# The first stage of a transformer layer kernel: both streams begun together, and the conditioning rows made by products

## The chip, the cores and the metric

The kernel runs on one NeuronCore of one Trainium2 chip. Its time is the device time of one execution in microseconds; three executions before the change took 1682.93, 1684.46 and 1685.36 us, so the median is 1684.46 us. A separate execution was profiled.

## The reference

One layer of a hybrid block works on 256 latent tokens `x` and 256 context tokens `ctx`, each of 2048 channels, in fp32. The part that matters here is its beginning: two conditioning vectors, `c` and `c_ctx`, go through silu and the matrix `w_ada` (2048 x 12288), which gives shift and scale for each stream; each stream is normed, scaled and shifted, and then multiplied by `w_in`.

```
sh1, sc1, ...    = split(silu(c) @ w_ada + b_ada, 6)
sh1c, sc1c, ...  = split(silu(c_ctx) @ w_ada + b_ada, 6)
h_l = modulate(rms_norm(x, norm1_w), sh1, sc1)
h_c = modulate(rms_norm(ctx, norm1_w), sh1c, sc1c)
... = split(h_l @ w_in),  split(h_c @ w_in)
x_new = x + g1 * merge(h_l, gla(...), diff_attention(...))
return x_new + g2 * conv_ffn(modulate(rms_norm(x_new, norm2_w), sh2, sc2))
```

What follows (a gated linear attention, a differential attention, the merge and a convolutional feed-forward net) is touched by neither diff nor order.

## The kernel before, in words

Activations lie with channels on the partitions: 16 tiles of 128 channels by 256 tokens for each stream. A product in fp32 is made of rounded halves: `hi` is the value rounded to fp32r, `lo` the rest, and hi*hi + hi*lo + lo*hi are summed.

The first stage runs 16 steps, one for each tile k of channels. A step needs shift and scale of its 128 channels for both streams. `ada_rows` gets them from PE: 16 products of the silu columns `ccol_s` with a 2 MB tile of `w_ada` (four loads `ada` of 512 KB), then a copy to SBUF on ACT (L525, tile `row`), two transposes on PE (L534) and, in `ada_cols`, three small operations on DVE (L536 to L538). `stage` then makes hi and lo of the normed tile: a scaling of x on DVE (L550), the rounding on ACT (L552), the difference on DVE (L556), for stream 0 (tile names `a`) and stream 1 (`c`). The step's part of `w_in`, 128 x 896 (`wraw<-in_w_sw`), is split into `whi` on ACT (L210) and `wlo` on DVE (L217). PE then multiplies: four row products of 128 tokens (`sweep_row`, banks 0 to 3, 512 columns), and three column products (`sweep_col`, banks 4 to 6, 256 columns for each stream). All of these stand in line L374 (`pinned`), so the tile names tell them apart. The ada products of step k+1 stand after the first row product of step k, and what follows from them is done while PE ends step k.

For three of the sixteen tiles (7, 11 and 15, `DOT_TILES`) shift and scale are not made on PE but by dots on DVE (`run_dots`, L412) of transposed tiles of `w_ada` (`ada<-in_w_ad1t`, 512 KB each) with a row of conditioning values that stands on all partitions: `cb` for stream 0, `cbc` for stream 1. The dots of steps 2 to 5 serve tile 7. `cb` is made by `cond_row`: full fp32 products of a broadcast column of `ccol_s` with the identity, copied from PSUM (L590). `cbc` is made another way: 1 MB of `c_ctx` is loaded by a broadcast (128 times the same row), ACT makes its silu factor in three operations a half (L433 to L435), and POOL multiplies (L436).

Before the steps stands the norm: squares of x on ACT and DVE (L491, L493), partly added on DVE (L497, L498), summed over channels by full fp32 products with `ones`, and the root on ACT and DVE (L511 to L515). Stream 0 is loaded, normed and multiplied first; stream 1 follows while step 0 is under way, so `cond_row` and the sums of squares are spread between the products of step 0.

The order on each engine in this stage is the order of the code (`keep_in_program_order`); behind it a scheduler orders the rest. All loads of the stage go through SP's queue (L346) in the order of the code, at most eight at a time; a load also waits until its buffer is free. The ada loads share a ring of 11 buffers (`SLOTS`), the w_in tiles one of four.

Of the kernel before, what the change touches and what calls it, by code (L numbers as in the profile page):

```python
# [44 lines left out]
LATE_ADA = {13: 1, 14: 2}  # L45
GATE_ADA = [0.25] * 4 + [0.5] * 16 + [1] * 12
# [30 lines left out]
def _lay_out(i):  # L77
# [6 lines left out]
    a["c_ctx"] = np.ascontiguousarray(np.asarray(i["c_ctx"])[None])  # L84
# [66 lines left out]
def layer_kernel(tc, I, out):  # L151
# [3 lines left out]
    with es:  # L155
# [213 lines left out]
        with tc.tile_pool(name="first", bufs=1) as p1:  # L369
# [54 lines left out]
            silu_steps = []  # L424

            def load_ctx_row():

                ordered_dma(cbc, I["c_ctx"].to_broadcast([P, D]))
                for q in range(2):
                    x = cbc[:, q * 1024:(q + 1) * 1024]  # L430
                    t = p1.tile([P, 1024], F32, tag="ada", bufs=SLOTS, name="silu")
                    silu_steps.extend([
                        lambda x=x, t=t: kept(S.activation(t, x, AF.Exp, scale=-1.0)),  # L433
                        lambda x=x, t=t: kept(S.activation(t, t, AF.Ln, bias=1.0)),
                        lambda x=x, t=t: (kept(S.activation(t, t, AF.Exp, scale=-1.0)),  # L435
                                          kept(G.tensor_tensor(x, x, t, op=ALU.mult)))])  # L436

# [14 lines left out]
            load_x(0)  # L452
            load_ada(0)
            load_sweep(0)
            load_x(1)

# [11 lines left out]
            logs = kept(act_table("natural_log_exp_and_others", silus))  # L468
            b1 = p1.tile([P, KT], F32, name="b1")
# [38 lines left out]
            def root(s, o):  # L508

                z, t = z1[:, s * T:(s + 1) * T], p1.tile([P, T], F32, tag="zt", bufs=2, name="zt")  # L510
# [75 lines left out]
            ss = sweep[4][:, :T], sweep[2][:, :T]  # L586
            rows = sweep[0], sweep[5], sweep[3], sweep[3]

            def cond_copy(q, copy):
                kept(copy(cb[:, q * 512:(q + 1) * 512], rows[q]))  # L590

            for q in range(2):
                cond_row(q, rows[q])
            for j in range(2):
                squares(0, j)
                added_squares(0, j)
                summed_squares(0, j, ss[0], j == 0, False, 1)
            squares(0, 2)
            squares(0, 3)
            added_squares(0, 2)  # L600
            summed_squares(0, 3, ss[0], False, False, 4)
            summed_squares(0, 2, ss[0], False, True, 1)
            for q in range(2):
                cond_copy(q, S.copy)
            root(0, ss[0])
            row, lows = ada_rows(0), []
            ws = sweep_splits(0, lows)
            m = ada_cols(0, row)
            cond_row(2, rows[2])
            stage(0, m, (0,), lows)  # L610
            for t in range(2):
                sweep_row(0, ws[0], t)
            for g in range(3):
                sweep_col(0, ws[1], g, (0,))
            for j in range(4):
                squares(1, j)
                if j < 3:
                    added_squares(1, j)
                summed_squares(1, j, ss[1], j == 0, j == 3, 1 if j < 3 else 4)
            cond_copy(2, V.tensor_copy)  # L620
            cond_row(3, rows[3])
            root(1, ss[1])
            cond_copy(3, S.copy)
            stage(0, m, (1,))
            row, lows = ada_rows(1), []
            load(2)
            load_ctx_row()
            nxt = sweep_splits(1, lows)
            sweep_row(0, ws[0], 2)
            m = ada_cols(1, row)  # L630
            sweep_row(0, ws[0], 3)
            stage(1, m, lows=lows)
            for g in range(3):
                sweep_col(0, ws[1], g, (1,))
            for k in range(1, KT):
# [4 lines left out]
                if k + 1 < KT:  # L640
                    load_halves(k + 1)
# [20 lines left out]
                for g in range(3):  # L662
                    sweep_col(k, ws[1], g)
# [774 lines left out]
```

## Time and profile before

| | |
|---|---|
| median of three executions | 1684.46 us |
| the profiled execution | 1686.63 us |
| its span | 1684.8 us |
| PE busy | 1662.6 us (99%) |
| DVE, ACT, POOL busy | 1308.4, 983.6, 349.3 us |
| first stage, to the last product of step 15 | 138.3 us |
| moved by DMA | 371.87 MB, mean 221 GB/s |

A row of the timeline has the start and length in us, the engine, the line of the kernel, the operation, what it writes and reads with shapes, how many were merged into the row, and in brackets how long the engine was idle before it and what ended that. PE's matmuls are pipelined, so one lasts longer than the distance to the next one; the distance of the starts is what a product costs. A product in full fp32 shows as two records.

### The profile page before, as it was taken

Reading aid. Unit: us, or ns where it says so; the run is one execution under the profiler, and the core shown is the slowest. Engines: PE = TensorE matmul, PEld = TensorE weight load, DVE = VectorE, ACT = ScalarE, POOL = GpSimd, SP = SyncE. Lnnn points to the kernel's source line nnn. Section 1 sums busy time; section 2 is a strip of 40 time slices with the busy share of each in tenths; the row PEclk is TensorE's granted clock in tenths of the full one; section 3 lists DMA queues with packets and bytes.
Section 4 is the critical chain, followed back from the end, with each engine's and each line's share of the span. In section 5 each row is a group of like instructions: output and inputs, shape, how many; then the busy total and the mean of one; then the engine's idle time right before and its main releaser. Section 6 shows DMA issues by size and latency. Waiting matters only on the chain.

```text
span 1684.8 us, 28432 instructions
## 1 busy us (share of the span) xinstructions
PE 1662.6 (99%) x10006; PEld 1436.7 (85%) x10006; DVE 1308.4 (78%) x2480; ACT 983.6 (58%) x1983; POOL 349.3 (21%) x442
## 2 busy tenths in 40 slices
PE   7999999999999999999999999999999999999998
PEld 5679999998788888888888998888888888888887
DVE  5788867768787988788998797878888787755655
ACT  5335555756355777666665686666666666544443
POOL 0101313132210000001324200222222222684000
PEclk9999999999999999999999999999999999999999
DMA  9996644436554555687887666677777776676664
GB/s 384 406 376 195 219 151 137 143 101 213 175 188 152 179 192 191 205 291 272 271 269 249 183 200 219 226 228 236 240 236 236 226 239 214 207 219 208 217 194 143
DMA packets 110975, 371.87 MB, mean 221 GB/s; under 512 B 14448, under 2 KB 19568, under 8 KB 110704
## 3 DMA queue, kind: packets, MB, share of 16 engines
q1 hardware_dynamic: 102256, 363.56, 65.1%
q10 hardware_dynamic: 4032, 4.37, 0.8%
q0 software_dynamic: 4544, 2.14, 0.6%
q8 instruction: 78, 1.28, 0.3%
q14 instruction: 65, 0.53, 0.1%
HBM read 365.78 MB, written 2.10 MB: 218 GB/s over the span
## 4 chain that ended last, share of the span: by engine, by line
PE 95%; DVE 2%; DMA 1%; issue 1%; ACT 1%; DVEq 0%; ACTq 0%
PE down L1390 14%; PE upg L268 9%; PE upv L268 9%; PE gate L268 7%; PE upv L270 5%; PE upg L270 5%; PE sweep L374 5%; PE gate L270 4%; PE mix L268 4%; PE mix L270 2%; PE pgb L268 2%; PE pga L268 2%; PE dk L339 2%; PE dk L338 2%; PE dk L337 2%; PE dvb L285 2%
## 5 line engine op out<-in xcount | busy, mean ns | idle before, releaser
L210 ACT CAST whi<-wraw 128x512 fp32r<-128x512 f32 (+2 forms) x1004 | 605.7, 608 | 391.0 <-DVE wlo L217 111.5
L217 DVE TENSOR_TENSOR wlo<-wraw,whi 128x512 fp32r<-128x512 f32 (+2 forms) x932 | 639.1, 694 | 222.2 <-ACT whi L210 209.1
L268 PE MATMUL upg<-a,whi 128*128 128x512 f32 x656 | 229.0, 391 | 0.0
L268 PE MATMUL upv<-a,whi 128*128 128x512 f32 x656 | 228.9, 391 | 0.0
L1390 PE MATMUL down<-whi,g 128*128 128x512 f32 x704 | 216.9, 389 | 0.0
L270 PE MATMUL upv<-a,wlo 128*128 128x256 f32 x656 | 183.0, 280 | 0.0
L270 PE MATMUL upg<-a,wlo 128*128 128x256 f32 x656 | 182.8, 280 | 0.0
L217 POOL TENSOR_TENSOR wlo<-wraw,whi 128x512 fp32r<-128x512 f32 x72 | 100.6, 1397 | 387.6 <-ACT whi L210 379.1
L268 PE MATMUL gate<-a,whi 128*128 128x512 f32 x512 | 179.8, 397 | 0.0
L362 DVE CUSTOM_DVE_ANT_0 araw<-araw,cb 128x1024 f32<-128x1024 f32 x128 | 161.6, 1265 | 13.8 <-DMA araw<-in_w_ada 13.8
L1390 PEld LDWEIGHTS down<-whi,g 128*128 128x128 f32 x704 | 132.1, 188 | 27.5
L268 PEld LDWEIGHTS upv<-a,whi 128*128 128x128 f32 x656 | 122.3, 187 | 26.4
L268 PEld LDWEIGHTS upg<-a,whi 128*128 128x128 f32 x656 | 122.4, 187 | 26.4
L270 PE MATMUL gate<-a,wlo 128*128 128x256 f32 x512 | 140.0, 284 | 0.0
L1390 PE MATMUL down<-wlo,g 128*128 128x512 f32 x352 | 137.0, 389 | 0.0
L270 PEld LDWEIGHTS upv<-a,wlo 128*128 128x128 f32 x656 | 124.1, 189 | 0.5
L270 PEld LDWEIGHTS upg<-a,wlo 128*128 128x128 f32 x656 | 124.1, 189 | 0.5
L268 PEld LDWEIGHTS gate<-a,whi 128*128 128x128 f32 x512 | 94.4, 188 | 19.6 <-issue 0.7
L270 PEld LDWEIGHTS gate<-a,wlo 128*128 128x128 f32 x512 | 96.5, 188 | 5.6 <-issue 1.8
L268 PE MATMUL mix<-a,whi 128*128 128x512 f32 x256 | 88.8, 397 | 0.0
L1390 PEld LDWEIGHTS down<-wlo,g 128*128 128x128 f32 x352 | 66.1, 188 | 13.6
L1363 POOL DMA_DIRECT2D row<-turned x128 | 69.3, 550 | 28.3 <-DVE turned L1359 16.7
(361 smaller groups left out, 3448.4 us busy)
## 6 DMA issues: line engine op xcount, KB each, us to landing
wraw<-in_w_up SPq DMA_DIRECT2D x164, 512.0 KB, 4.5
araw<-in_w_ada SPq DMA_DIRECT2D x128, 512.0 KB, 5.0
wraw<-in_w_down SPq DMA_DIRECT2D x88, 512.0 KB, 4.3
wraw<-in_w_gate SPq DMA_DIRECT2D x64, 512.0 KB, 4.5
wraw<-in_w_in SPq DMA_DIRECT2D x58, 512.0 KB, 4.3
ada<-in_w_ad SPq DMA_DIRECT2D x52, 512.0 KB, 9.8
wraw<-in_w_proj SPq DMA_DIRECT2D x32, 512.0 KB, 4.7
wraw<-in_w_out SPq DMA_DIRECT2D x32, 512.0 KB, 4.8
```

The source lines that it names most:

```text
L210: copied[0] = S.copy(hi[:, :n], raw)
L217: i = e.tensor_tensor(lo[:, :n], raw, hi[:, :n].bitcast(F32), op=ALU.subtract)
L268: i = PE.matmul(b.rearrange("p (a b) -> p a b", a=2), whi[:, sl], acts[k], start=first, stop=last)
L270: i = PE.matmul(b[:, T:], wlo[:, sl], acts[k][:, 1, :], start=False, stop=last)
L285: return PE.matmul(o, hi[k][:, ts], wlo[:, sl], start=False, stop=last)
L337: PE.matmul(o, whi[:, sl], hi[k], start=first and j == 0, stop=False)
L338: PE.matmul(o, whi[:, sl], lo[k], start=False, stop=False)
L339: i = PE.matmul(o, wlo[:, sl], hi[k], start=False, stop=last and j == 1)
L362: i = V.tensor_tensor_reduce(raw, raw, cb[:, q * 1024:(q + 1) * 1024], 1.0, 0.0, op0=ALU.mult, op1=ALU.add, accum_out=ada2[:, j, q:q + 1])
L374: return kept(PE.matmul(*args, **kw))
L1363: nc.gpsimd.dma_start(to[32 * (q % 4):32 * (q % 4 + 1), :, 32 * p:32 * (p + 1)], turned[32 * p:32 * (p + 1), :, 32 * q:32 * (q + 1)])
L1390: i = PE.matmul(banks[h][t][n], g[:, a, ts], w[n][b], start=k == 0 and (a, b) == (1, 0), stop=k == FT - 1 and b == 1)
```

## The change

Stream 1 is loaded right behind stream 0 and ahead of the first ada tiles; both are normed together, with one root over 512 columns, and step 0 is run for both streams like any other. The row `cbc` is no longer loaded: it is made like `cb`, by products with the identity, from the silu column of stream 1. These products are now made with rounded operands: the column is split into `chi` and `clo`, and each is multiplied by the rounded identity `identr`, so there are 64 rounded products where there were 16 in full fp32. The eight results are copied to `cb` and `cbc` by ACT and DVE. The three silu steps of each half on ACT and the two products on POOL are gone. A table `ROWS_AT` says after how many of a step's seven products the ada products of the next step stand: four in steps 0 and 1, two in step 2, one in the others; the transposes stand two products later, at most before the sixth.

On SP the order of the loads was this (`x` the streams, `ada` the tiles of `w_ada`, `wraw` those of `w_in`):

```order
L346 DMA x<-in_xl 128x1024 x4
L346 DMA ada<-in_w_ad 128x1024 x4
L346 DMA wraw<-in_w_sw 128x896
L346 DMA x<-in_xc 128x1024 x4
L346 DMA ada<-in_w_ad 128x1024 x4
L346 DMA wraw<-in_w_sw 128x896 x2
L346 DMA ada<-in_w_ad 128x1024 x4
L346 DMA cbc<-in_c_ctx 128x2048
L346 DMA wraw<-in_w_sw 128x896
```

and now:

```order
L346 DMA x<-in_xl 128x1024 x4
L346 DMA x<-in_xc 128x1024 x4
L346 DMA ada<-in_w_ad 128x1024 x4
L346 DMA wraw<-in_w_sw 128x896
L346 DMA ada<-in_w_ad 128x1024 x4
L346 DMA wraw<-in_w_sw 128x896 x2
L346 DMA ada<-in_w_ad 128x1024 x4
L346 DMA wraw<-in_w_sw 128x896
```

The ctx tiles moved ahead of five loads, and the broadcast row is gone; the rest of SP's order is as it was.

On PE the program began like this (`sweep_133` to `139` are banks 0 to 6, `ab` the bank of the ada products):

```order
L374 MATMUL sweep_133<-ident,ccol_s 128x128 x4
L374 MATMUL sweep_138<-ident,ccol_s 128x128 x4
L374 MATMUL sweep_137<-sq,ones 128x256 x7
L374 MATMUL ab<-ada,ccol_s 32x256 x16
L534 MATMUL ab<-ident,row 128x128 x2
L374 MATMUL sweep_136<-ident,ccol_s 128x128 x4
L374 MATMUL sweep_133<-whi,a_222 128x512
L374 MATMUL sweep_133<-wlo,a_222 128x512
```

Now 48 rounded products on six banks stand first (the last two are shown; banks are 139 to 145), then the sums of both streams, 16 more rounded products on banks 2 and 3, and the ada products. This is the end of that piece:

```order
L374 MATMUL sweep_145<-identr,chi 128x128
L374 MATMUL sweep_145<-identr,clo 128x128
L374 MATMUL sweep_143<-sq,ones 128x256 x14
L374 MATMUL sweep_141<-identr,chi 128x128
L374 MATMUL sweep_141<-identr,clo 128x128
...
L374 MATMUL ab<-ada,ccol_s 32x256 x16
L526 MATMUL ab<-ident,row 128x128 x2
L374 MATMUL sweep_139<-whi,a_313 128x512
L374 MATMUL sweep_139<-wlo,a_313 128x512
```

Everything PE has to do for both norms and all conditioning rows now stands ahead of the first row product. On POOL two products left the queue, with nothing else moved; before:

```order
L471 TENSOR_SCALAR b_129<-vec 128x16
L472 TENSOR_SCALAR nw_130<-vec 128x16
L436 TENSOR_TENSOR cbc<-cbc,silu 128x1024 x2
L419 TENSOR_TENSOR sums_96<-sums_96 128x4
L420 TENSOR_SCALAR shsc<-sums_96,b_129,nw_130 128x2
L421 TENSOR_SCALAR shsc<-sums_96,vec 128x2
```

From step 3 on, and through all later stages, the order on each of the five queues is the same before and after. The diff, cut to its core:

```diff
+ROWS_AT = [4, 4, 2, 1]
...
-            silu_steps = []
-
-            def load_ctx_row():
-
-                ordered_dma(cbc, I["c_ctx"].to_broadcast([P, D]))
-                for q in range(2):
-                    x = cbc[:, q * 1024:(q + 1) * 1024]
-                    t = p1.tile([P, 1024], F32, tag="ada", bufs=SLOTS, name="silu")
...
             load_x(0)
+            load_x(1)
             load_ada(0)
             load_sweep(0)
-            load_x(1)
-
             load_ada(1)
             load_sweep(1)
...
+            identr = p1.tile([P, P], F32R, name="identr")
+            chi, clo = [p1.tile([P, KT, 2], F32R, name=n) for n in ("chi", "clo")]
+            kept(V.tensor_copy(chi, ccol_s[:, :, :2]))
+            kept(V.tensor_tensor(clo, ccol_s[:, :, :2], chi.bitcast(F32), op=ALU.subtract))
+            kept(V.tensor_copy(identr, ident))
...
-            def cond_row(q, b):
+            def cond_row(s, q, b, copy):
 
                 for u in range(4):
-                    pinned(b[:, u * P:(u + 1) * P], ccol_s[:, 4 * q + u, 0:1].to_broadcast([P, P]), ident,
-                           start=True, stop=True)
+                    for i, c in enumerate((chi, clo)):
+                        pinned(b[:, u * P:(u + 1) * P], c[:, 4 * q + u, s:s + 1].to_broadcast([P, P]), identr,
+                               start=i == 0, stop=i == 1)
+                return lambda: kept(copy((cb, cbc)[s][:, q * 512:(q + 1) * 512], b))
...
+            ss = sweep[4]
+            copies = [cond_row(0, q, sweep[q], S.copy if q < 2 else V.tensor_copy) for q in range(4)]
+            copies += [cond_row(1, q, sweep[5 + q], S.copy) for q in range(2)]
+            for s in range(2):
+                o = ss[:, s * T:(s + 1) * T]
...
+            for c in copies[2:4]:
+                c()
+            copies += [cond_row(1, q, sweep[q], V.tensor_copy) for q in range(2, 4)]
+            for c in copies[6:]:
+                c()
+            root(ss)
+            for c in copies[:2]:
+                c()
             row, lows = ada_rows(0), []
...
+            nxt = sweep_splits(0, lows)
+            stage(0, ada_cols(0, row), lows=lows)
+            for c in copies[4:6]:
+                c()
+            for k in range(KT):
                 ws = nxt
...
-                for t in range(4):
-                    if turned and t == 1:
+                at = ROWS_AT[min(k, len(ROWS_AT) - 1)]
+                steps = [lambda t=t: sweep_row(k, ws[0], t) for t in range(4)]
+                steps += [lambda g=g: sweep_col(k, ws[1], g) for g in range(3)]
+                for i, step in enumerate(steps):
+                    if turned and i == at:
                         row = ada_rows(k + 1)
-                        for step in silu_steps[:2]:
-                            step()
-                        del silu_steps[:2]
-                    if turned and t == 3:
+                    if turned and i == min(at + 2, 5):
                         cols = ada_cols(k + 1, row)
-                    sweep_row(k, ws[0], t)
+                    step()
```

More of the change, by code (lines that the diff above doesn't have):

```diff
@@ L506, in summed_squares, with root @@
                     pinned(o, ones.bitcast(F32), p, start=first and i == 0, stop=last and i == n - 1)
-            def root(s, o):
-                z, t = z1[:, s * T:(s + 1) * T], p1.tile([P, T], F32, tag="zt", bufs=2, name="zt")
+            def root(o):
+                z, t = z1, p1.tile([P, 512], F32, name="zt")
                 kept(S.activation(z, o, AF.Ln, scale=1.0 / D, bias=epsb))
@@ L585, in layer_kernel @@
             pin[0] = True
[L586 to L605, printed above, removed]
-            row, lows = ada_rows(0), []
[L607 to L635, printed above, removed]
+            ss = sweep[4]
+            copies = [cond_row(0, q, sweep[q], S.copy if q < 2 else V.tensor_copy) for q in range(4)]
+            copies += [cond_row(1, q, sweep[5 + q], S.copy) for q in range(2)]
@@ new lines, in layer_kernel @@
+            for s in range(2):
+                o = ss[:, s * T:(s + 1) * T]
+                for j in range(2):
+                    squares(s, j)
+                    added_squares(s, j)
+                    summed_squares(s, j, o, j == 0, False, 1)
+                squares(s, 2)
+                squares(s, 3)
+                added_squares(s, 2)
+                summed_squares(s, 2, o, False, False, 1)
+                summed_squares(s, 3, o, False, True, 4)
+            for c in copies[2:4]:
+                c()
@@ L639, in layer_kernel @@
                 load(k + 2)
-                if k + 1 < KT:
+                if more:
                     load_halves(k + 1)
@@ L650, in layer_kernel @@
                     m = dotted(k + 2)
-                for t in range(4):
-                    if turned and t == 1:
+                at = ROWS_AT[min(k, len(ROWS_AT) - 1)]
[3 more added lines that the diff above has]
+                    if turned and i == at:
                         row = ada_rows(k + 1)
-                        for step in silu_steps[:2]:
-                            step()
-                        del silu_steps[:2]
-                    if turned and t == 3:
+                    if turned and i == min(at + 2, 5):
                         cols = ada_cols(k + 1, row)
-                    sweep_row(k, ws[0], t)
+                    step()
                 if turned:
                     stage(k + 1, cols)
-                for g in range(3):
-                    sweep_col(k, ws[1], g)
                 for _ in range(LATE_ADA.get(k - 1, 0)):
```

6 lines of the change are left out of this document (removed).

## The prediction

> **What bounds the kernel now.** First the page: which engine is full, and what the chain that ended last is made of.
>
> ```profile
> PE 1662.6 (99%) x10006; PEld 1436.7 (85%) x10006; DVE 1308.4 (78%) x2480; ACT 983.6 (58%) x1983; POOL 349.3 (21%) x442
> PE   7999999999999999999999999999999999999998
> DMA  9996644436554555687887666677777776676664
> PE 95%; DVE 2%; DMA 1%; issue 1%; ACT 1%; DVEq 0%; ACTq 0%
> ```
>
> PE bounds the program, except in the first slice. Only the first three slices have full DMA engines, and the change lies in them. So I cut the first stage into its steps, at the start of each step's first row product on PE (31.24 is step 1, 138.30 the end of step 15). The columns are the stretch and its length, the busy time of PE, PEld, DVE, ACT and POOL (instructions in brackets), the granted clock, the DMA share and GB/s.
>
> ```profile
> 6.30:31.24 24.94, 22.40 (x158) 17.27 (x159) 14.91 (x34) 15.56 (x34) 1.22 (x2) 1.00 1.03 409
> 31.24:39.13 7.89, 7.89 (x65) 5.50 (x65) 4.18 (x12) 4.26 (x8) 0.00 (x0) 1.00 1.02 413
> 39.13:50.46 11.33, 7.90 (x66) 5.25 (x65) 7.72 (x14) 4.06 (x8) 2.64 (x1) 1.00 1.03 407
> 50.46:60.72 10.26, 9.17 (x64) 6.12 (x65) 7.93 (x14) 4.22 (x8) 2.42 (x1) 0.83 1.03 408
> 60.72:67.93 7.21, 7.21 (x63) 5.39 (x64) 6.53 (x15) 3.02 (x7) 0.00 (x0) 1.00 1.02 406
> 67.93:75.14 7.21, 7.21 (x66) 5.43 (x65) 5.88 (x15) 1.84 (x5) 0.82 (x3) 1.00 1.03 409
> 75.14:138.30 63.16, 63.16 (x508) 50.53 (x507) 53.82 (x118) 22.03 (x46) 5.61 (x9) 1.00 0.90 336
> ```
>
> A step that waits for nothing takes 7.21 us, and from step 4 (60.72) on PE has no gap. Steps 2 and 3 take 11.33 and 10.26: 7.2 us above two clean steps. The PE timeline shows where.
>
> ```profile
> 43.07 0.64 PE L374 MATMUL ab<-ada,ccol_s 128*32 128x256 f32 x8 [0.64 <-DMA ada<-in_w_ad]
> 50.46 0.50 PE L374 MATMUL sweep<-whi,a 128*128 128x512 f32 x1 [2.10 <-ACT a L552]
> 51.41 3.47 PE L374 MATMUL ab<-ada,ccol_s 128*32 128x256 f32 x32
> 60.72 0.50 PE L374 MATMUL sweep<-whi,a 128*128 128x512 f32 x1 [1.09 <-ACT a L552]
> ```
>
> Step 2 waits for tiles of the ada weights, the last until 43.07; steps 3 and 4 begin late, since the normed x was late. Ahead of that wait stand these rows of DVE and POOL:
>
> ```profile
> 44.32 1.23 DVE L412 CUSTOM_DVE_ANT_0 junk<-ada,cb 128x1024 f32<-128x1024 f32 x1 [3.19 <-DMA ada<-in_w_ad1t]
> 45.74 3.18 DVE L412 CUSTOM_DVE_ANT_0 junk<-ada,cb 128x1024 f32<-128x1024 f32 x1 [0.18 <-DMA ada<-in_w_ad1t]
> 49.38 0.88 DVE L550 SCALAR_TENSOR_TENSOR x<-x,shsc,z 128x256 f32<-128x256 f32 x2
> 57.43 3.09 DVE L550 SCALAR_TENSOR_TENSOR x<-x,shsc,z 128x256 f32<-128x256 f32 x2
> 45.19 2.64 POOL L436 TENSOR_TENSOR cbc<-cbc,silu 128x1024 f32<-128x1024 f32 x1 [35.31 <-DMA wraw<-in_w_sw]
> 57.43 2.42 POOL L436 TENSOR_TENSOR cbc<-cbc,silu 128x1024 f32<-128x1024 f32 x1 [9.60 <-ACT silu L435]
> ```
>
> The same dot takes 1.23 and 3.18, the same pair of scalings 0.88 and 3.09: 2.0 and 2.2 us more, just while POOL multiplies the context row by its silu factor. The third loss is the clock:
>
> ```profile
> 48.23:51.64 3.41, 1.31 (x9) 0.64 (x11) 3.17 (x10) 1.74 (x4) 0.00 (x0) 1.00 1.02 407
> 51.64:55.06 3.42, 3.42 (x33) 1.55 (x26) 3.16 (x6) 0.22 (x2) 0.00 (x0) 0.50 1.03 406
> ```
>
> After a stretch in which PE worked 1.31 of 3.41 us, the next ran at half clock, and the 32 ada products of 51.41 took 3.47 us; at full clock they take 1.93 (row of 13.38 below).
>
> **The change, part by part.**
>
> *The context row's load goes.*
>
> ```profile
> cbc<-in_c_ctx SPq DMA_DIRECT2D x1, 1024.0 KB, 12.0
> ```
>
> It stands on SP's queue after the ada tiles of step 2. DMA is full at 407 GB/s, so its 1.05 MB is 2.6 us by which every later tile lands earlier. The last ada tile of step 3 comes at 40.5 instead of 43.07. After it the order has two dot halves, a sweep tile and four ada tiles (six of 1.28 and one of 1.12 us, 512 and 448 KB by 408 GB/s): 49.3 for step 4; with one half, 56.8 for step 5; with none, 63.1 for step 6. These are the floors of DMA.
>
> *The two POOL products go*, and with them six silu steps on ACT, worth nothing by themselves (ACT was busy 4.06 of 11.33 us and 4.22 of 10.26 there). DVE gets 4.2 us back; PE's two late starts (2.10 and 1.09) lose their cause, and so does the half clock that followed the first.
>
> *The first step waits for both streams.* Four tiles of ctx now stand before the ada tiles of step 0, 5.1 us of DMA. These rows price the new beginning:
>
> ```profile
> 6.30 3.75 PE L374 MATMUL sweep<-ident,ccol_s 128*128 128x128 f32 x16 [6.30 <-DMA ident<-in_ident]
> 13.38 1.93 PE L374 MATMUL ab<-ada,ccol_s 128*32 128x256 f32 x32
> 16.08 1.06 PE L374 MATMUL sweep<-ident,ccol_s 128*128 128x128 f32 x8
> 18.05 0.50 PE L374 MATMUL sweep<-whi,a 128*128 128x512 f32 x1 [0.92 <-ACT a L552]
> 19.37 0.40 PE L374 MATMUL sweep<-whi,a 128*128 128x512 f32 x1
> 19.60 0.28 PE L374 MATMUL sweep<-a,whi 128*128 128x256 f32 x1
> 19.72 0.28 PE L374 MATMUL sweep<-a,wlo 128*128 128x256 f32 x1
> 22.41 2.43 PE L374 MATMUL sweep<-sq,ones 128*128 128x256 f32 x10 [0.36 <-DVE sq L498]
> ```
>
> By DMA, step 0 moves from 18.05 to 23.2. Behind its first row product nothing but PE's own later work is queued. By PE, it waits for a queue: 64 rounded products of 128 columns, 28 records of the squares' sums (2.43/10, without its last tail some 0.22 each: 6.2), the ada products (1.93), and from their end to the first row product 2.74 (15.31 to 18.05).
>
> *The price p of one rounded product* is not in the trace: it has none with 128 moving columns. From below: 512 columns take 0.23 (19.37 to 19.60) and 256 take 0.12 (19.60 to 19.72), so 128 would take 0.06. From above: it goes no faster than the product in full precision, two records of 0.11 in the row of 16.08, 0.22. I take 0.09, between 0.06 and the nearest row, 0.12 at 256 columns, since each product also loads 128 columns of weights. At first PE runs at half speed (the row of 6.30: 0.22 a record where 16.08 has 0.11). I give that 4.2 us, a little more than this row's 3.75, from 6.5 (the casts of identity and halves come first) to 10.7; they do 2.1 us' worth. Step 0 then begins at 10.7 + 64p - 2.1 + 6.2 + 1.93 + 2.74 = 19.5 + 64p.
>
> That is 25.2 us with 0.09; with 0.06 it is 23.3, as by DMA; with 0.22 it is 33.6. The Trainium skill (TensorE: Matmul & The Clock Gate, Back-to-back issue gap) gives about 81 ns for a sustained pair of weight load and 128-column product; by it step 0 would begin at 24.7, an estimate from that page that changes the sum by 0.5 us.
>
> *The ada products of the next step stand later* in steps 0 to 2 (after four, four and two rows). Steps 0 and 1 then end on the chain behind them, and I give them the 7.89 of step 1 before; steps 2, 3 and 4 take 7.21, their DVE work (6.53 in the clean step) fitting in. With 25.2 they begin at 41.0, 48.2 and 55.4, and step 5 at 62.6. In steps 3 to 5 the last quarter of the ada products runs 2.4 us after the step's start (0.95 by the rows of 50.46 and 51.41, three quarters of 1.93), at 50.6, 57.8 and 65.0: behind the floors 49.3, 56.8 and 63.1.
>
> *At no cost* are the copies of the conditioning rows and the ring of ada slots.
>
> ```profile
> L590 ACT COPY cb<-sweep 128x512 f32<-128x512 f32 x3 | 1.6, 568 | 0.0
> ```
>
> The sums of squares end near 19.1 (25.2 less 2.74, 1.93 and the last 16 products' 1.44). The norm's root is five operations on 512 columns, some 0.6 us each by this row: 22.1, and it is wanted 1.08 before step 0 (49.38 to 50.46), at 24.1. Two copies stand ahead of the root on DVE and two wait for the last products there, two more stand on ACT behind it; 2.0 us of slack hold them, and beyond it they would move step 0 one for one. The ring has 11 slots: the twelfth ada tile needs one of step 0, free near 21.0, and ahead of it on DMA's queue stand 22 transfers, 27.7 us of work.
>
> **Sum.** Step 5 begins at 62.6 instead of 67.93: 5.3 us. From there the order on every engine is as before and PE has no gap, so the shift is carried. The profiled execution took 1686.63 (span 1684.8), 2.2 above the median of 1684.46; 5.3 less is 1681.3 for it and **1679.2** for the median. With 0.06, the floors of steps 4 and 5 take back 0.6 and 0.3 of the 1.9: 6.3 us, 1678.2. With 0.22 step 5 begins at 71.0: 3.1 us later.
>
> **Rivals.**
> 1. *The rounded products go at full precision's pace.* Then 64 of them replace 16 as dear, PE's queue alone decides, and the time is 1687.6, slower. It decides from p = 0.17, where 19.5 + 64p reaches 30.5. For it: no row has such a product. Against it: time falls with columns between 512 and 256 without a floor.
> 2. *The gain is partly spent again*: the 2.74 us before step 0, in which PE only turns two tiles, bring back the half clock (3.47 less 1.93, 1.5 us), and steps 0 and 1, waiting for the chain behind their late ada products, run 0.5 us longer each: 2.5 us, 1681.7. For it: a stretch 38% busy was enough at 48.23. Against it: the like gap from 15.31 left the clock at 1.00, though it held 1.06 us of products that now stand ahead of it. The skill (same page, What's actually happening) asks for an idle window of about 3.4 us on a free-running grid; read strictly this gap never brings the half clock, and the sum stays at 1679.2. The row of 48.23 differs: its window was not idle.
> 3. *It is given back later*: a stage paced by transfers or by DVE takes the shift up: 1684.5. For it: DVE is 78% busy. Against it: no later slice has PE below 9 tenths before the last, and DMA is mostly at 4 to 8 tenths.
>
> **How the numbers follow.** The forecast has 0.58, with its own range 1677.5 to 1681; rival 1 has 0.13, rival 2 0.17, rival 3 0.12. About 0.2%, 3.4 us, is what a measurement here can tell. Faster is the forecast and a third of rival 2, 0.64; within is the rest of 2, rival 3 and half of 1 (its 3.1 us lie at the limit), 0.29; slower 0.07. The range 1676.5 to 1685.0 takes in the lower bound of p with 1.7 us to spare, and rivals 2 and 3, and leaves out rival 1 and little else.
>
> **What would show it.** In the changed profile: the rounded products 0.06 to 0.12 us apart at full clock; step 0 near 25 and step 5 near 62.6; no dot (L412) above 1.3 us and no pair of scalings above 0.9 in steps 2 to 4; no half clock near 50; the first sweep products of steps 2 to 5 waiting under 0.5 us. Products 0.2 us apart, or a step 2 that starts after 44, prove it wrong; a first stage 5 us shorter with the same total proves rival 3.

## The result, and the profile after

| | before | after |
|---|---|---|
| median, 22 executions each | 1685.11 us (1682.93 to 1686.8) | 1687.62 us (1685.12 to 1690.73) |
| profiled execution, its span | 1686.63, 1684.8 us | 1686.85, 1684.9 us |
| step 0 begins | 18.05 us (stream 0 alone) | 31.69 us |
| step 5 begins | 68.08 us | 70.56 us |

The time after is 1.0016 of the time before, 95% interval 1.0009 to 1.0022: 2.5 us slower. The forecast was 1679.2, 8.4 us less, and the time lies above the range. Step 5 begins 2.48 us later than before, where 5.3 us earlier were forecast. The prediction's windows end before's step 4 at 67.93, but before's timeline has the first row product of step 5 at 68.08:

```profile
68.08 0.40 PE L374 MATMUL sweep<-whi,a 128*128 128x512 f32 x1
```

So step 4 took 7.36 us there and not 7.21, and step 5, to 75.29, took 7.21. The next two lines are of after's page; the prediction shows the same two of before.

```profile
PE 1667.0 (99%) x10038; PEld 1443.7 (86%) x10038; DVE 1304.9 (77%) x2484; ACT 978.2 (58%) x1975; POOL 338.5 (20%) x440
...
PE 97%; DVE 2%; DMA 1%; ACT 0%; issue 0%; DVEq 0%; ACTq 0%
```

The two POOL products are gone and PE has more of the chain than before, but PE also has 4.4 us more busy time. The second view is again the first stage cut at the first row product of each step. Its first row runs from the first rounded product to step 0; its last two rows are the stretch just ahead of a half-clock stretch, and that stretch itself.

```profile
6.60:31.69 25.09, 22.79 (x127) 20.12 (x127) 13.18 (x26) 12.57 (x24) 0.90 (x2) 1.00 1.03 408
31.69:40.95 9.26, 8.97 (x64) 6.59 (x65) 4.22 (x12) 3.17 (x8) 0.00 (x0) 0.82 0.90 323
40.95:48.77 7.82, 7.54 (x65) 5.46 (x65) 3.42 (x10) 2.21 (x6) 0.00 (x0) 1.00 0.96 343
48.77:56.14 7.37, 7.37 (x65) 5.46 (x65) 6.07 (x14) 2.47 (x7) 0.00 (x0) 1.00 0.95 335
56.14:63.36 7.22, 7.22 (x67) 5.42 (x65) 6.38 (x16) 2.80 (x7) 0.00 (x0) 1.00 1.02 411
63.36:70.56 7.20, 7.20 (x66) 5.42 (x65) 5.80 (x14) 2.30 (x5) 0.00 (x0) 1.00 1.03 410
28.15:31.56 3.41, 1.24 (x18) 0.43 (x10) 2.40 (x8) 1.95 (x6) 0.00 (x0) 1.00 1.02 406
31.56:34.97 3.41, 3.28 (x8) 2.53 (x9) 2.95 (x6) 2.36 (x6) 0.00 (x0) 0.50 1.03 408
```

From step 2 on everything is near the forecast: no stall, and 7.37, 7.22 and 7.20 us a step (7.21 forecast), where before steps 2 and 3 took 11.33 and 10.26. All that was gained there and more is lost ahead of step 1. A warning on the first row: its 1.00 in the column of the granted clock says nothing, since the trace has no record of the clock before 21.32 us, where full clock begins. The clock ahead of that is read from the distance of like products, in PE's timeline:

```profile
6.60 0.48 PE L374 MATMUL sweep<-identr,chi 128*128 128x128 f32 x1 [6.60 <-DVE identr L458]
6.88 0.42 PE L374 MATMUL sweep<-identr,clo 128*128 128x128 f32 x1
7.09 0.41 PE L374 MATMUL sweep<-identr,chi 128*128 128x128 f32 x1
...
16.48 0.41 PE L374 MATMUL sweep<-identr,chi 128*128 128x128 f32 x1
16.69 0.41 PE L374 MATMUL sweep<-identr,clo 128*128 128x128 f32 x1
16.91 8.45 PE L374 MATMUL sweep<-sq,ones 128*128 128x256 f32 x28
25.00 0.41 PE L374 MATMUL sweep<-identr,chi 128*128 128x128 f32 x1
25.25 0.27 PE L374 MATMUL sweep<-identr,clo 128*128 128x128 f32 x1
25.36 0.28 PE L374 MATMUL sweep<-identr,chi 128*128 128x128 f32 x1
...
27.02 1.93 PE L374 MATMUL ab<-ada,ccol_s 128*32 128x256 f32 x32
31.69 0.79 PE L374 MATMUL sweep<-whi,a 128*128 128x512 f32 x1 [1.81 <-ACT a L544]
```

The first 48 rounded products stand 0.21 us apart to their end, 10.31 us in all; the last 16 of the same form stand 0.11 apart. So PE ran at half clock through all of the first group and 4.4 us into the sums of squares, 14.7 us after its first product. I had given the half clock 4.2.

The profiled execution of after is none the less only 0.2 us longer than that of before. One reason is a stretch of half clock that before's execution had much later and after's had not; before by windows:

```profile
457.83:461.24 3.41, 3.41 (x12) 2.84 (x12) 3.27 (x11) 1.90 (x4) 0.00 (x0) 0.50 0.18 73
```

That is up to 1.7 us; the rest of the difference I did not locate. The execution of before that was profiled lay 1.5 us above the median of its 22. The comparisons below therefore go by medians, and by the start of step 5 in the profiles.

### The profile page after: what moved, and what is told of

It reads as the page before. It is cut to its first block, busy times and chain, and to the rows that moved or that the text cites. A ratio compares the mean times of both kernels' runs of the same rounds, so it can differ in the third digit from the quotient of the medians.

```text
span 1684.9 us, 28493 instructions
## 1 busy us (share of the span) xinstructions
PE 1667.0 (99%) x10038; PEld 1443.7 (86%) x10038; DVE 1304.9 (77%) x2484; ACT 978.2 (58%) x1975; POOL 338.5 (20%) x440
## 4 chain that ended last, share of the span: by engine, by line
PE 97%; DVE 2%; DMA 1%; ACT 0%; issue 0%; DVEq 0%; ACTq 0%
PE down L1358 14%; PE upg L268 9%; PE upv L268 9%; PE gate L268 7%; PE sweep L374 6%; PE upv L270 5%; PE upg L270 5%; PE gate L270 4%; PE mix L268 4%; PE mix L270 2%; PE pgb L268 2%; PE pga L268 2%; PE dk L339 2%; PE dvb L285 2%; PE dk L338 2%; PE dvb L284 2%
## 5 line engine op out<-in xcount | busy, mean ns | idle before, releaser
L268 PEld LDWEIGHTS upv<-a,whi 128*128 128x128 f32 x656 | 122.4, 187 | 26.6
```

The lines of the kernel that those rows point to most:

```text
L268: i = PE.matmul(b.rearrange("p (a b) -> p a b", a=2), whi[:, sl], acts[k], start=first, stop=last)
```

## The experiments

The first expectations state their theories by letters. A is the one that held: rounded products of 128 columns with weights of their own do not bring the clock up, so that they and the sums behind them run at half clock. B is that the queue of products is too long by itself and the clock rises at a time of its own; C is that the wait for both streams costs the time. Each median is one of 11 executions, except after's (22), that of the first products twice (4) and the last row's (8). The medians stand beside a median of before of 1685.0, 1685.09 or 1685.03 us (first four runs, next four, last three). All kernels but one are edits of after. Steps are given by the start of their first row product.

| kernel | step 0 | step 5 | median | ratio to before, 95% |
|---|---|---|---|---|
| after | 31.69 | 70.56 | 1687.62 | 1.0016 (1.0009 to 1.0022) |
| rows in full precision | 27.02 | 64.74 | 1683.02 | 0.9989 (0.9981 to 0.9998) |
| first products twice | 41.37 | 80.12 | 1696.75 | 1.0071 (1.0057 to 1.0085) |
| products of ones ahead | 25.02 | 62.70 | 1682.07 | 0.9983 (0.9974 to 0.9992) |
| 16 products moved into the gap | 27.45 | 65.20 | 1681.90 | 0.9984 (0.9975 to 0.9992) |
| ones ahead and moved | 24.90 | 62.68 | 1681.22 | 0.9983 (0.9974 to 0.9992) |
| the same, full precision | 25.05 | 62.76 | 1680.85 | 0.9976 (0.9967 to 0.9984) |
| the load back | 24.91 | 64.84 | 1684.25 | 0.9993 (0.9984 to 1.0002) |
| POOL products back | 24.87 | 63.30 | 1682.19 | 0.9987 (0.9978 to 0.9996) |
| wide rounded products | 27.39 | 65.17 | 1683.19 | 0.9988 (0.9979 to 0.9997) |
| before, ones ahead | 17.88 | 66.42 | 1684.49 | 0.9996 (0.9987 to 1.0005) |
| full precision, other rows in the gap | 23.95 | 62.20 | 1680.82 | 0.9973 (0.9963 to 0.9983) |

The median less the start of step 5 is 1616.6 to 1619.4 us in all twelve, where step 5 ranges over 18 us: what happens ahead of step 5 is carried to the end, but for some 2 us. The seven kernels that begin step 5 before 65 us lie at 1618.1 to 1619.4, before and the other five at 1616.6 to 1618.1, so the earlier ones lose some of their gain behind step 5. One place shows in three of their profiles, a wait of PE for DVE near 443 us; with the ones ahead and the products moved it reads, in PE's waits from 400 to 500 us:

```profile
PE sc L871 <- DVE e L903: 2.1, 1, 2.1
```

In the same kernel with full precision it takes 2.3 us and in the last kernel of the table 2.4, but 0.4 in after, 0.8 in before, and 0.7 with the ones alone, where step 5 begins at the same time. What makes it longer was not tried.

### Rows in full precision

```
-  for i, c in enumerate((chi, clo)):
-      pinned(b[:, u * P:(u + 1) * P], c[:, 4 * q + u, s:s + 1].to_broadcast([P, P]), identr, start=i == 0, stop=i == 1)
+  pinned(b[:, u * P:(u + 1) * P], ccol_s[:, 4 * q + u, s:s + 1].to_broadcast([P, P]), ident, start=True, stop=True)
```

The three casts of the halves and of the identity are gone too. PE has as many records: a product in full precision shows as two.

> The change with its 64 rounded products put back to 32 in full fp32 (the casts of halves and identity gone). They are 64 records again, 0.11 us apart at full clock like the rounded ones. Theory A (clock): rounded products of 128 columns keep PE too idle to raise the clock, which is why it stood at half until 21.3 us in the changed profile; full products raise it near 10.7 as before, and step 0 begins near 26.5 instead of 31.7: 5 us less, about 1682.5. Theory B (queue): 64 records of 0.11 us are too long a queue, and the late clock was where its window happened to fall: nothing moves, 1687.6. Theory C (waiting for both streams costs the time): 1687.6 too.

PE's timeline of this kernel:

```profile
6.35 8.24 PE L374 MATMUL sweep<-ident,ccol_s 128*128 128x128 f32 x48 [6.35 <-DMA ident<-in_ident]
14.43 6.21 PE L374 MATMUL sweep<-sq,ones 128*128 128x256 f32 x28
20.48 1.95 PE L374 MATMUL sweep<-ident,ccol_s 128*128 128x128 f32 x16
22.35 1.93 PE L374 MATMUL ab<-ada,ccol_s 128*32 128x256 f32 x32
```

The first 48 records take 8.08 us instead of 10.31, the sums 6.05 instead of 8.09, and the trace has full clock from 11.91. The last 16 take 1.87, against 2.02 of the rounded ones at the same clock: per row the two forms cost nearly the same, so the rounded product has little handicap but the clock (and no merit either). Step 5 comes 5.8 us sooner and the median is 4.6 us below after's. A holds, and B and C, which expected no gain, fall. Undoing this part alone brings the kernel 2.0 us below before.

### The first rounded products made twice

```
-  for i, c in enumerate((chi, clo)):
+  for i, c in enumerate((chi, clo) * (1 if s and q > 1 else 2)):
       pinned(..., identr,
-             start=i == 0, stop=i == 1)
+             start=i % 2 == 0, stop=i % 2 == 1)
```

Each of the first 48 products is made a second time into the same place, so the values are the same.

> The change with the first 48 rounded products made twice. Theory A: the clock stays at half through all 96, so 48 more of 0.213 us: 10.2 us more, about 1697.8, and the clock rises only after 27 us. Theory B: the clock rises at about the same time as in the changed profile (21.3), so the rest of the added products costs 0.11 each and the sums behind them run at full clock: 5.6 us more, about 1693.

```profile
26.45 0.41 PE L374 MATMUL sweep<-identr,chi 128*128 128x128 f32 x1
26.66 0.41 PE L374 MATMUL sweep<-identr,clo 128*128 128x128 f32 x1
26.88 8.16 PE L374 MATMUL sweep<-sq,ones 128*128 128x256 f32 x28
```

And the stretch of all 96, by windows (the clock column's 1.00 again stands for no record):

```profile
6.34:26.88 20.54, 20.54 (x97) 20.54 (x97) 9.11 (x16) 7.76 (x14) 0.66 (x2) 1.00 1.03 406
```

PE is busy for 20.54 of 20.54 us, and its last two products still stand 0.21 apart: the clock never rose. It did at 30.72, 3.8 us after the sums had begun. A clock that rises at a time of its own would have made the added products half as dear, 1693; A expected 1697.8, and the median of four executions is 1696.75.

### Products of ones ahead

```
   pin[0] = True
+  for i in range(14):
+      pinned(ab[:, :P], ones.bitcast(F32), ones.bitcast(F32), start=True, stop=True)
```

These products in full precision fill the 6 us in which PE waits for the first casts; nobody reads what they write.

> The change with 14 products of ones by ones in full fp32 ahead of the rounded ones, from about 1 us on, while PE has nothing to do. Theory A: the clock is full by 7 to 8 us; if rounded products hold it (the window that lost it before had PE 38% busy, they keep it about half busy), step 0 begins near 24.6 and the time falls by 6 us or more, about 1681; if they don't hold it, the clock falls again within 3.4 us and little is won (1686 to 1687). Theory B and C: 1687.6.

```profile
1.06 6.13 PE L374 MATMUL ab<-ones 128*128 128x128 f32 x28 [1.06 <-DVE ones L174]
6.94 0.31 PE L374 MATMUL sweep<-identr,chi 128*128 128x128 f32 x1
7.08 0.27 PE L374 MATMUL sweep<-identr,clo 128*128 128x128 f32 x1
...
25.02 0.49 PE L374 MATMUL sweep<-whi,a 128*128 128x512 f32 x1 [1.79 <-ACT a L544]
```

Full clock from 6.83, and the rounded products stand 0.11 apart from the first on: once the clock is up, 5.4 us of them hold it. Step 0 begins at 25.02 and step 5 at 62.70, where the forecast had 25.2 and 62.6. The median, 1682.07, stays 2.9 us above the forecast's; the executions reach from 1679.4 (mean granted clock 1.000) to 1685.0 (0.997).

### Sixteen products moved into the gap

```
-  copies += [cond_row(1, q, sweep[5 + q], S.copy) for q in range(2)]
   ...
-  stage(0, ada_cols(0, row), lows=lows)
+  m = ada_cols(0, row)
+  copies = [cond_row(1, q, sweep[5 + q], S.copy) for q in range(2)]
+  stage(0, m, lows=lows)
```

Half of the second row's products now stand behind the transposes of step 0, where PE waited for the first scaled x.

> The change with 16 of the first 48 rounded products (the first half of stream 1's row) moved behind the transposes of step 0, into the 2.3 us in which PE waits for the first normed tile. Theory A: the queue ahead of step 0 is shorter by 16 products at half clock, 3.4 us, and the half clock that the empty stretch brought back at 31.6 in the changed profile (1.4 us) stays away: 4 to 5 us less, about 1683. Theory B: 16 products of 0.11, 1.8 us less, 1685.8, and nothing more. Theory C: 1687.6.

The gap in this kernel, by windows:

```profile
25.20:27.45 2.25, 2.18 (x19) 2.04 (x19) 1.58 (x6) 1.44 (x4) 0.00 (x0) 1.00 1.04 405
```

PE is busy for 2.18 of the 2.25 us ahead of step 0, no half clock follows it, and steps 0 and 1 take 8.13 and 7.83 us (9.26 and 7.82 in after). The sums begin at 13.35 instead of 16.91, and the clock is full at 16.39. Step 5 gains 5.4 us, the median 5.7.

### Both together, with rounded and with full products

The edits of the two runs above in one kernel; the second kernel has the full products of the first run as well.

> The change with both edits: 14 full fp32 products of ones ahead, and 16 rounded products moved behind the transposes of step 0. The clock theory adds them: the clock is full by 7 us and no empty stretch ahead of step 0 brings the half clock back, so step 0 begins near 23.0, where the loads of both streams end it, step 5 near 61.8 (by DMA's floors) instead of 70.6 in the changed profile and 67.93 before. About 1679, 6 us below the kernel before, with a narrow spread of executions. If the half clock was not the cause, the two gains don't add and it stays near 1682.

> The same with all conditioning rows in full fp32 instead of rounded halves: the same number of records at the same distance. If rounded products at full clock are neither dearer nor cheaper than full ones (0.11 us), and the clock holds with both, this equals the run with rounded products within 1 us, about 1679. If rounded products still cost clock now and then, this one is faster by the share of executions that lose it, 0.5 to 1.5 us.

The gains did not add, and the first expectation was missed: step 0 begins at 24.90 and 25.05, no sooner than with the ones alone, and the medians stay 2 us above 1679. That expectation took this outcome as a sign against the clock. The trace shows another reason, a new wait in PE's timeline of the kernel with rounded products:

```profile
11.74 3.29 PE L374 MATMUL sweep<-sq,ones 128*128 128x256 f32 x14 [0.33 <-DVE sq L490]
16.14 2.43 PE L374 MATMUL sweep<-sq,ones 128*128 128x256 f32 x10 [1.11 <-DVE sq L490]
```

PE now comes to the sums before their squares are there. In after this wait did not show, since the slow products covered it. The two kernels lie within 0.4 us of each other: rounded or full makes no difference that shows once the clock is up. The one with full products is 1680.85, 4.2 us below before.

### The load back, and the POOL products back

Both are the kernel "ones ahead and moved" with one removed part returned. The first loads 1 MB of `c_ctx` by a broadcast at its old place, into two slots of the ada ring that nobody reads; the second makes two products of 128x1024 on POOL beside the dots of steps 2 and 3, also read by nobody.

```
+  if k == 1:
+      for q in range(2):
+          t = p1.tile([P, 1024], F32, tag="ada", bufs=SLOTS, name="back")
+          ordered_dma(t, I["c_ctx"][:, q * 1024:(q + 1) * 1024].to_broadcast([P, 1024]))
   load(k + 2)
```

```
+  if (n, u, q, t) in ((0, 0, 1, 0), (0, 1, 0, 0)):
+      kept(G.tensor_tensor(scratch[q], h, h, op=ALU.mult))
```

> The kernel with both edits, with the broadcast load of the context row put back in its old place on the queue (1 MB, into two slots of the ada ring, read by nobody). Theory: with a beginning this early the ada tiles of steps 3 to 6 bind PE, so the load costs its 2.6 us of DMA time: steps 4 to 6 begin 2 to 2.6 us later, about 1681.3. Rival: PE has slack behind DMA there, and the time stays at 1679.

> The kernel with both edits, with two POOL products of 128x1024 fp32 put back beside dots of steps 2 and 3 (they multiply a dot's tile by itself into ring slots that nobody reads). Theory: POOL and DVE shut each other out, the two dots beside them take 2 to 3 us instead of 1.22 as before, the normed tiles of steps 3 and 4 come late and PE waits: 2 to 4 us more, 1681 to 1683. Rival: the long dots of the kernel before had another cause; dots stay at 1.22 and the time at 1679.

With the load, PE waits for the ada weights again, above all its queue of weight loads (PEld); these waits from 38 to 66 us are absent without the load (what waited for what, us in total, times, longest):

```profile
PEld ab L375 <- DMA ada<-in_w_ad: 2.3, 3, 1.1
PE ab L375 <- DMA ada<-in_w_ad: 0.6, 1, 0.6
```

Step 5 begins 2.2 us later (64.84 against 62.68) and the median is 3.0 us up, on both sides of the 2.6 us of transfer that the prediction gave it. With the POOL products, the timelines of DVE and POOL read:

```profile
42.80 1.22 DVE L414 CUSTOM_DVE_ANT_0 junk<-ada,cb 128x1024 f32<-128x1024 f32 x1
44.06 2.79 DVE L414 CUSTOM_DVE_ANT_0 junk<-ada,cb 128x1024 f32<-128x1024 f32 x1
50.36 1.22 DVE L414 CUSTOM_DVE_ANT_0 ada<-ada,cbc 128x1024 f32<-128x1024 f32 x1
51.51 2.91 DVE L414 CUSTOM_DVE_ANT_0 junk<-ada,cb 128x1024 f32<-128x1024 f32 x1
...
43.24 2.53 POOL L413 TENSOR_TENSOR scratch<-ada 128x1024 f32<-128x1024 f32 x1 [34.26 <-PE ab L374]
50.42 2.91 POOL L413 TENSOR_TENSOR scratch<-ada 128x1024 f32<-128x1024 f32 x1 [4.65 <-DMA ada<-in_w_ad1t]
```

A dot that begins while POOL multiplies takes 2.79 or 2.91 us; the two that had begun before the product take 1.22, though the product overlaps them. Each long dot ends 1.1 us after the product (46.85 after 45.77, 54.42 after 53.33, and 48.92 after 47.83 by the prediction's rows of before), as if it did its work only then. DVE loses 3.3 us, but step 5 only 0.6 and the median 1.0, less than I had expected: in this kernel the two steps have slack on DVE (6.07 of 7.37 and 6.38 of 7.22 us busy in the rows of after). Before, the load had already made these steps late.

### Wide rounded products

```
+  w = 1 if u == 3 else 2
-  pinned(b[:, u * P:(u + 1) * P], c[...].to_broadcast([P, P]), identr, start=i == 0, stop=i == 1)
+  pinned(b[:, u * P:(u + w) * P], c[...].to_broadcast([P, P]), identr.to_broadcast([P, w, P]), start=i == 0, stop=i == 1)
```

(Shapes shortened.) Three of each four products run over the identity twice, 256 columns; the second half is overwritten by the next product, so the rows are the same. This tells two readings of A apart: that the clock goes by how much of the time the array streams columns, or by something else in rounded products.

> The change with three of each four rounded products 256 columns wide instead of 128 (the identity is read twice, and what the second half writes is overwritten by the next product; results are the same). Form, halves and number of products stay. Theory A1: PE's clock rises by how much of the time the array streams columns, and a rounded product of 128 columns streams half of its time while it waits for its own weights; with 256 columns it streams nearly all of it, so the clock rises near 11 to 12 us, step 0 begins near 27 and the time is about 1683, although the products stream twice the columns. Theory A2: rounded products as such, or those with one broadcast column as weights, don't count; the clock stays at half until the sums, step 0 begins near 31.7 or later, 1687.6 or more.

```profile
7.28 0.41 PE L374 MATMUL sweep<-identr,clo 128*128 128x256 f32 x1
7.49 0.41 PE L374 MATMUL sweep<-identr,chi 128*128 128x256 f32 x1
...
12.39 0.28 PE L374 MATMUL sweep<-identr,clo 128*128 128x256 f32 x1
12.51 0.28 PE L374 MATMUL sweep<-identr,chi 128*128 128x256 f32 x1
```

At half clock a product of 256 columns takes the 0.21 us that one of 128 took in after. The count of products, the weights and the pace are the same; only the columns of three in four are double, and now the clock is full from 12.36 while the products still run. Step 0 begins at 27.39 and the median is 1683.19, as A1 expected. If a column takes the same time in both kernels, after's products left the array without columns half of the time or more, though the trace calls PE busy throughout. That the clock goes by streaming is what these runs bear out; what the chip counts, the trace doesn't show.

### Before, with the ones ahead

The products of ones, put ahead of before's first products.

> The kernel before with the same 14 products of ones ahead. There PE's first products wait for nothing that comes late and the first step waits for its loads, so the clock theory expects no gain: step 0 of stream 0 near 18.0 as before, 1685 within 0.7 us. If a full clock at the start is worth 4 us by itself wherever it is put, this falls to 1681.

Its clock is full from 4.86 (before: from 10.68), and still the median moves only from 1685.03 to 1684.49, which the interval doesn't tell from nothing. PE now waits for squares (0.45 and 0.36 us) and for the last ada tile (0.36 us) ahead of step 0, which begins at 17.88 instead of 18.05: most of what PE gained goes into waits. Warming up is worth something only where PE sets the start.

### Full precision, ones ahead, other rows in the gap

```
-  stage(0, ada_cols(0, row), lows=lows)
+  m = ada_cols(0, row)
+  copies = [cond_row(1, q, sweep[q], S.copy) for q in range(2, 4)]
+  stage(0, m, lows=lows)
```

Here the second half of the second row stands in the gap, so that the ada products follow right on the sums, and the six other copies go ahead of the root.

> The change with full fp32 rows, the 14 products of ones ahead, and another 16 records in the stretch behind the transposes of step 0: those of the second half of stream 1's row, which stood between the sums and the ada products; their copies go from DVE to ACT behind the first normed tiles. The ada products then follow the sums at once: step 0 begins near 23.1 instead of 24.9 to 25.1. DMA's floors for the ada tiles of steps 4 to 6 take back part: step 5 near 61.7 instead of 62.7, about 1 us less than with the rows moved otherwise, 1680.

```profile
12.07 6.46 PE L374 MATMUL sweep<-sq,ones 128*128 128x256 f32 x28
18.46 1.50 PE L374 MATMUL ab<-ada,ccol_s 128*32 128x256 f32 x24
20.59 0.64 PE L374 MATMUL ab<-ada,ccol_s 128*32 128x256 f32 x8 [0.63 <-DMA ada<-in_w_ad]
```

The ada products begin 1.8 us sooner than with rounded products and both edits, and then wait for their last tile: step 0 has come to the transfers. It begins at 23.95, step 5 at 62.20, and the median is 1680.82, 4.2 us below before and 6.8 below after. This and the kernel with full products, both edits, are the fastest of the study and not to be told apart.

## Why the prediction was wrong

**The step that failed is the sentence "I give that 4.2 us".** I took the length of the half clock from before's first products, and took it for a time from PE's start on. It hangs on what PE does: products in full precision raise it, rounded products of 128 columns don't, and after ran at half clock for 14.7 us. The table puts the terms against after's trace.

| term | forecast | measured |
|---|---|---|
| first 48 rounded products, half clock for 4.2 us | 6.42 us | 10.31 |
| sums of squares | 6.2 | 8.09 |
| last 16 products | 1.44 | 2.02 |
| ada products and the chain to step 0 | 1.93 + 2.74 | 1.93 + 2.74 |
| step 0 begins | 25.2 | 31.69 |
| step 0 | 7.89 | 9.26 |
| steps 1 to 4 | 29.52 | 29.61 |
| step 5 begins | 62.6 | 70.56 |

Of the 6.5 us at step 0 the half clock is 4.9: 48 times 0.102 (0.213 less 0.111) and 2.07 in the sums (8.09 less 6.02 with the ones ahead) make 7.0, of which 2.1 were forecast. The price of a product is 1.3: 0.111 instead of 0.09, 64 times. The rest is 0.3.

**The price p** lay within its bounds, but at the upper neighbour, 0.12 at 256 columns, and not between it and 0.06: at full clock a product of 128 columns with weights of its own costs 0.111, about as much as one of 256 (0.12 between the last rows of the wide products). The Trainium skill's figure (TensorE: Matmul & The Clock Gate, Back-to-back issue gap), 81 ns, was further off; the measurement decides. In the expression 19.5 + 64p the price alone gives 26.6 for step 0. With the ones ahead both errors can be seen to cancel nearly: without any half clock and with p = 0.111 the same terms give 6.94 + 7.1 + 6.2 + 1.93 + 2.74 = 24.9, measured 25.02, beside the forecast's 25.2.

**Rival 2's first half came true** and cost 1.1 us: half clock came back behind the gap ahead of step 0, after a stretch with PE busy for 1.24 of 3.41 us, and step 0 took 9.26 us, where the kernels without it take 8.1. I had argued against it that the like gap before had left the clock alone. Its second half, steps 0 and 1 longer by themselves, did not: without half clock they take 8.1 and 7.8 us, 15.9 for the 15.8 forecast.

**Rival 1 met the time, but not by its mechanism.** It had 1687.6, from products that cost 0.22 each at any clock. They cost that only at half clock. The test that I had named, products 0.2 us apart, did prove the forecast wrong, but can't tell the two apart; the last 16, 0.11 apart, can.

**What was right.** The load's price and the floors: no tile is waited for in steps 2 to 5 of after, and returning the load costs 2.2 us at step 5. POOL beside DVE: after's dots and scalings from 0 to 75 us, by groups, are

```profile
L412 DVE CUSTOM_DVE_ANT_0 junk<-ada,cb 128x1024 f32<-128x1024 f32 x4 | 4.9, 1220 | 0.0
L412 DVE CUSTOM_DVE_ANT_0 ada<-ada,cbc 128x1024 f32<-128x1024 f32 x4 | 4.8, 1221 | 0.0
L542 DVE SCALAR_TENSOR_TENSOR x<-x,shsc,z 128x256 f32<-128x256 f32 x12 | 5.3, 480 | 0.0
```

none above 1.3 us, as forecast. There is no half clock near 50, steps 1 to 4 came out within 0.1 us in sum, and the shift is carried to the end, so rival 3 falls for this change: step 5 moved by 2.48 us, the medians by 2.51. Of the miss of 8.4 us, 7.96 stand at step 5. Two smaller terms nearly account for the rest: before's median is 1685.11 by 22 executions and not 1684.46 by three (0.65 more), and with 68.08 the forecast's 62.6 was 5.5 us earlier and not 5.3 (0.2 less).

One more size was off, on the other side. The sum was made against an execution with two stretches of half clock, one of them near 50, whose end I counted as a gain of 1.5 us for the median. Executions of before may not all have it: with the ones ahead, the profiled execution had none there and began step 5 at 66.42. Only one execution of before itself was profiled, so this is inferred. Part of the 5.3 us was then no gain for the median, and the kernel with the ones ahead, whose step 5 lies within 0.1 us of the forecast's, has a median 2.9 us above the forecast. Its profiled execution, at full clock from 6.83 to 1675.9, took 1679.37: 7.3 us less than before's, of which 5.4 stand at step 5 and up to 1.7 are before's stretch at 457.83.

## What to carry to other kernels

Where PE works alone at the start of a program or after a gap, price the clock with the products: ask what each product streams and how long, not whether the trace calls PE busy. Narrow products with weights of their own cost as much as products twice as wide and may keep the clock down for as long as they last; put wide or full-precision work ahead of them (unread products in idle time will do), and put work that is due anyway into gaps. A price measured next to other work, like the 4.2 us here, is carried over with what made it.

## What the runs showed of the hardware beyond expectation

**The clock goes in steps of 3.41 us.** In after's trace full clock lasts from 21.32 to 31.56, three times 3.41, and half clock one time; the first products made twice show the same pattern from 30.72. In these two kernels full clock begins behind the first such stretch that lies wholly in the sums of squares (17.91 to 21.32 and 27.31 to 30.72); with sixteen products moved, a stretch with 0.4 us of narrow products and 3.0 of sums was enough (12.98 to 16.39). With the Trainium skill (TensorE: Matmul & The Clock Gate, What's actually happening) the traces agree on a free-running window of about 3.4 us. They do not bear out that so much sustained activity is enough: 10.3 and 20.5 us of gapless narrow products did not raise the clock.

**A stretch need not be idle to bring half clock back.** 36% busy was enough in after, 38% in before and 45% in the kernel with the first products twice; 57% and 67% held the clock in two others. After's row stands above, before's in the prediction; these are the stretches around the gap ahead of step 0 in the kernels with the first products twice, the rows in full precision, and the ones ahead, in this order:

```profile
37.55:40.96 3.41, 1.53 (x24) 0.59 (x14) 2.41 (x7) 1.95 (x6) 0.00 (x0) 1.00 0.69 220
```

```profile
25.56:28.97 3.41, 1.95 (x7) 1.29 (x8) 3.15 (x9) 2.60 (x7) 0.00 (x0) 1.00 1.04 411
```

```profile
23.89:27.30 3.41, 2.28 (x8) 1.61 (x9) 2.79 (x8) 1.87 (x4) 0.00 (x0) 1.00 1.03 407
```

Only the first of the three was followed by half clock. What a gap of some 2.5 us costs thus depends on how the grid of 3.41 us falls across it. A second place like this lies between 452 and 470 us, where PE waits 2.1 us for DVE in each of the thirteen profiles. Six of them have a stretch of half clock there (before, before with the ones ahead, the rows in full precision, the first products twice, the wide products and the load back), the other seven have none. The executions of one kernel differ by 2 to 6 us. In after this goes with the mean granted clock: the four executions with 1.000 took 1685.1 to 1685.6 us, the twelve with 0.998 took 1686.7 to 1690.7. It is not all, since with sixteen products moved ten executions with 1.000 still spread over 2.2 us. Where in the other executions the clock was lost is not on record.
